# Moving the second FFN's down weight sums from VectorE into adding transfers between DRAM tensors

## The chip, the cores and the metric

The kernel runs on one core of a Trainium2 chip (trn2). The metric is the device time of one execution in microseconds. The kernel before takes 1124.04 us (median of 3 executions, 1123.24 to 1124.38). A difference of about 0.2% (2.25 us) is the least that can be told from no change.

The engines are called as in the profile: PE (TensorE, matmul), PEld (its weight loads), DVE (VectorE), ACT (ScalarE), POOL (GpSimd), SP (SyncE, which here issues nearly all transfers). "L121" is line 121 of the kernel before; the changed kernel has 18 to 24 lines more above most of its code, so there the same line has a higher number.

## The reference

One decoder block on 512 tokens of width 1024, in float32: a SwiGLU feed-forward layer (FFN), a token mixer with two branches, and a second SwiGLU FFN, each between two RMS norms.

```python
def swiglu(x, w_gu, w_down):
    g, u = jnp.split(x @ w_gu, 2, axis=-1)
    return (jax.nn.silu(g) * u) @ w_down

def hybrid_mixer(u, ...):
    z = u @ w_in
    gate_br, x_br, q, k, v, g_lru, g_attn = jnp.split(z, IN_SPLITS, axis=-1)
    xc = causal_depthwise_conv(x_br, conv_w, conv_b)
    y_lru = rg_lru(xc, ...) * jax.nn.gelu(gate_br)
    ...                                   # rotary q and k
    y_attn = sliding_window_attention_with_sinks(q, k, v, attn_sinks)
    merged = jax.nn.sigmoid(g_lru) * (y_lru @ w_proj_lru) + jax.nn.sigmoid(g_attn) * (y_attn @ w_proj_attn)
    return merged @ w_out

def reference(x, ...):
    h = x
    for l in range(DEPTH):                # DEPTH = 1
        f = swiglu(rms_norm(h, ffn1_pre_g[l]), ffn1_w_gu[l], ffn1_w_down[l])
        h = h + MACARON_SCALE * rms_norm(f, ffn1_post_g[l])
        m = hybrid_mixer(rms_norm(h, mix_pre_g[l]), ...)
        h = h + rms_norm(m, mix_post_g[l])
        f = swiglu(rms_norm(h, ffn2_pre_g[l]), ffn2_w_gu[l], ffn2_w_down[l])
        h = h + MACARON_SCALE * rms_norm(f, ffn2_post_g[l])
    return h
```

The inner width of both FFNs is 2816, that is 22 blocks of 128.

## The kernel before, in words

**Products.** Every float32 product is made of three matmuls on a high and a low part of each operand (`mm3`, L150 to L152): high by high, high by low, low by high. A weight block of 128 by 1024 comes from DRAM into one of six buffers (`wload`, L111, issued by SP), ACT writes its high part (L120) and DVE its low part (L121); this is `wsplit`. A fixed list, `worder`, holds all weight blocks in the order in which they are used. Blocks are split two ahead of their use (`AHEAD = 2`), and a block's load is issued once the block six places before it is split (`RAHEAD = 6`). A block of 128 by 1024 feeds 24 matmuls of 512 columns.

**Stages, in order of time in the profiled execution.** First gate and up products of FFN 1 (to about 246 us); down product of FFN 1 (to about 356 us, with the norm that follows); the mixer (to about 785 us); gate and up of FFN 2 (to about 990 us); down of FFN 2 and the last norm (to the end). Inside the mixer come the k and v group, the x group (eight chunks, whose convolution and recurrence are `lru_chunk`), four q chunks (`turn`: rotary), eight chunks of the GeLU gate (`gate_chunk`), four more q chunks, and then eight times a merge gate and a projection (`sig_gate`, `project`), with the attention heads (`attend`) begun beside them.

**The down products and their weight sums.** The down products are made in Strassen's scheme with seven products instead of eight (`strassen_out`). Four of the seven need sums of the quarters of the down weights. With 11 pairs of blocks `c` and `c + 11`, and the halves b11, b12 (block `c`, left and right) and b21, b22 (block `c + 11`), the four sums are s0 = b11 + b12, s1 = s0 + b22, s2 = s1 + b21 and s3 = b12 + b22. They lie in a scratch tensor in DRAM (`t_spill`, one of 128 x 4 x 512 for each pair and FFN), and `worder` takes them from there later, as weight blocks of the products q5, p6, q4 and p7. The sums of both FFNs are formed by the generator `weight_sums` during the first gate and up stage: SP loads two blocks (L283), DVE adds four times (L293), SP stores the sums (L294), 22 times, 11 for each FFN. Only the first FFN's sums are needed soon after.

**What sets the order.** The program is written as interleaved generators: `start` begins one, each call of `tick` lets the running ones count down, and a `yield n` waits for n ticks. In the mixer there is a tick after each product of 24 matmuls (about 5.4 us). The framework then orders the instructions of each engine with a timeline of its own; each engine runs its own list strictly in order, and waits at an instruction until what it needs is there. Buffers come from pools and are handed round: `t2` has 11 buffers of 128 x 512 (the tiles xc, xch, xcl, tr, qa, qb, qw, gp, gls and the attention's ph, pl and c), `t4` has 4 of 128 x 1024 (the attention's scores s, among others), `b8` has 19 of 128 x 2048. The instruction that first writes a new tile into a buffer waits until all readers of the old tile are done.

**POOL before.** POOL does little: the small powers of the norms (L187), and one copy of the sinks into each of the 16 score tiles (`attend`, L918), which waits until the tile's buffer is free.

Of the kernel before, what the change touches and what calls it, by code (L numbers as in the profile page):

```python
# [11 lines left out]
ALU = mybir.AluOpType  # L12
# [4 lines left out]
P = 128  # L17
# [14 lines left out]
KH = KF // 2  # L32
# [11 lines left out]
def hybrid_block_kernel(ctx, tc, x, xt, gcol, gains, gu_first, gu1, dn1, w_x, w_gate, w_kv, w_q, w_gl, w_ga, w_pl,  # L44
# [22 lines left out]
    def b8(name, shape, dtype=F32):  # L67
        return big.tile(shape, dtype, name=name, tag="b8")
# [201 lines left out]
        A.copy(ph[:, i, :], p[:, i, :])  # L270
        V.tensor_tensor(out=pl[:, i, :], in0=p[:, i, :], in1=ph[:, i, :].bitcast(F32), op=ALU.subtract)

    def weight_sums(wait):
        yield wait
        todo_ = [(dn, scratch[f], f, c) for f, dn in enumerate((dn1, dn2)) for c in range(KH)]
        loaded = []

        def load():
            if len(loaded) < len(todo_):
                dn, _, f, c = todo_[len(loaded)]  # L280
                raw = b8(f"tr{f}{c}", [P, 2, 1024])
                for i in range(2):
                    SP.dma_start(raw[:, i, :], dn[c + i * KH])  # L283
                loaded.append(raw)

        load()
        yield 2
        for n, (dn, scr, f, c) in enumerate(todo_):
            raw = loaded[n]
            b11, b12, b21, b22 = (raw[:, i, hc] for i in range(2) for hc in (slice(0, 512), slice(512, 1024)))  # L290
            ts = b8(f"ts{f}{c}", [P, 4, 512])
            for o, a, b in ((0, b11, b12), (1, ts[:, 0], b22), (2, ts[:, 1], b21), (3, b12, b22)):
                V.tensor_tensor(out=ts[:, o], in0=a, in1=b, op=ALU.add)  # L293
            SP.dma_start(scr[c], ts)  # L294
            load()
            yield 1 + n % 4 // 2

    class Blocks:
        def __init__(self, u, name, base, ps):
# [130 lines left out]
    def gate_up(u, name, rows=None, marks=None):  # L430
# [52 lines left out]
        if rows is None:  # L483
            stops.append(base + 2 * block_pairs[0])
            blocks = Blocks(u, name, base, ps)
            extra = blocks.operands(marks)
            first_four(u, f"{name}f", done, marks, extra)
            for _ in extra:
                pass
            blocks.prepare(block_pairs[0])  # L490
        else:
            start(weight_sums(6))
        for j in range(2 if rows is None else 0, KF):
            bb = []
            if j in block_pairs:
# [295 lines left out]
    def lru_chunk(c, b, a4, m4, bx4, last):  # L791
        i = c % 4
        xc = t2(f"xc{c}")
        A.activation(xc, b, AF.Identity, scale=vec[:, 3, c:c + 1], bias=vec[:, 4, c:c + 1])
        for s in range(1, 4):
            V.scalar_tensor_tensor(out=xc[:, s:], in0=b[:, :T - s], scalar=vec[:, 3 - s, c:c + 1], in1=xc[:, s:],
                                   op0=ALU.mult, op1=ALU.add)
        xh, xl = t2(f"xch{c}", F32R), t2(f"xcl{c}", F32R)
        A.copy(xh, xc)
        trail.append(V.tensor_tensor(out=xl, in0=xc, in1=xh.bitcast(F32), op=ALU.subtract))  # L800
        yield LRU_LAG[c // 4]
        cb = slice(c * P, (c + 1) * P)
        br, bi = bank(f"r{c}"), bank(f"i{c}")
        mm3(br, bdt[0][:, 0, cb], bdt[0][:, 1, cb], xh, xl, True, True)
        mm3(bi, bdt[1][:, 0, cb], bdt[1][:, 1, cb], xh, xl, True, True)
        tr = t2(f"tr{c}")
        A.activation(tr, br, AF.Tanh, scale=0.5, bias=hb[:, 0, c:c + 1])
        ti = bx4[:, i, :]
        A.activation(ti, bi, AF.Tanh, scale=0.5, bias=hb[:, 1, c:c + 1])
        V.scalar_tensor_tensor(out=ti, in0=ti, scalar=1.0, in1=xc, op0=ALU.add, op1=ALU.mult)  # L810
        A.activation(a4[:, i, :], tr, AF.Exp, scale=nsp[:, c:c + 1], bias=nsp[:, c:c + 1])
        A.activation(tr, tr, AF.Tanh, scale=nsp[:, c:c + 1], bias=nsp[:, c:c + 1])
        A.activation(m4[:, i, :], a4[:, i, :], AF.Square)
        V.scalar_tensor_tensor(out=m4[:, i, :], in0=m4[:, i, :], scalar=1.0, in1=tr, op0=ALU.add, op1=ALU.mult)
        if not last:
            return
        yield LRU_END[c // 4]
        V.tensor_scalar_min(m4, m4, 0.0)
        A.activation(m4, m4, AF.Sqrt, scale=-0.25)
        for i in range(4):  # L820
            yield 1
            with tc.issue_after(gated[-1].ins) if gated else nullcontext():
                V.tensor_tensor(out=bx4[:, i, :], in0=bx4[:, i, :], in1=m4[:, i, :], op=ALU.mult)
                V.tensor_tensor_scan(out=m4[:, i, :], data0=a4[:, i, :], data1=bx4[:, i, :], initial=0.0,
                                     op0=ALU.mult, op1=ALU.add)
# [3 lines left out]
    def x_group(gi):  # L829
        a4, m4, bx4 = (b8(f"{n}{gi}", [P, 4, T]) for n in ("la", "lm", "lb"))  # L830
        hl.append(m4)
        cr = range(4 * gi, 4 * gi + 4)
        for c in cr:
            w = wget()
            b = bank(f"x{c}")
            feat_chunk(b, w, u2, ALL)
            tick()
            start(lru_chunk(c, b, a4, m4, bx4, c == cr[-1]))

    def qkv_block(b, t, kk, w):  # L840
        for k2 in range(2):
# [57 lines left out]
    def turn(b, name, qh, ql):  # L899
        za, zb, zw = (t2(f"{n}{name}") for n in ("qa", "qb", "qw"))  # L900
        V.tensor_tensor(out=za, in0=b, in1=csq[:, 0], op=ALU.mult)
        trail.append(V.tensor_tensor(out=zb, in0=b, in1=csq[:, 1], op=ALU.mult))
        for i in range(4):
            SP.dma_start(zw[(i ^ 1) * 32:(i ^ 1) * 32 + 32, :], zb[i * 32:i * 32 + 32, :])
        yield 2
        with tc.issue_after(trail[-1].ins) if trail else nullcontext():
            V.tensor_tensor(out=za, in0=za, in1=zw, op=ALU.add)
        A.copy(qh, za)
        V.tensor_tensor(out=ql, in0=za, in1=qh.bitcast(F32), op=ALU.subtract)

    def attend(gi, n, jh, qt, kp, vt, y):
        nm = f"at{gi}{n}{jh}"
        nk = 1 if n == 0 else 2
        W = nk * P
        keys = slice((n - nk + 1) * P, (n + 1) * P)
        s = t4p.tile([P, 4, W + 1], F32, name=f"{nm}s", tag="t4")
        ns = nsink.rearrange("p (a r j i) -> p a r j i", a=2, r=2, j=2)[:, gi, :, jh, :]
        G.tensor_copy(s.rearrange("p (r i) w -> p r i w", r=2)[:, :, :, W], ns)  # L918
        mx, ss = sm(f"{nm}m", 4), sm(f"{nm}ss", 4)
        bs = [bank(f"{nm}b{r}") for r in range(2)]  # L920
        rows = [slice(r * HD, (r + 1) * HD) for r in range(2)]
# [44 lines left out]
    def gate_chunk(c):  # L966
# [6 lines left out]
        A.activation(p, b, AF.Square)  # L973
        gated.append(V.scalar_tensor_tensor(out=p, in0=p, scalar=1.0 / GELU_C, in1=b, op0=ALU.add, op1=ALU.mult))
        trail.append(gated[-1])
        A.activation(p, p, AF.Tanh, scale=SQRT_2_PI * GELU_C)
        V.scalar_tensor_tensor(out=p, in0=p, scalar=1.0, in1=b, op0=ALU.add, op1=ALU.mult)
        V.scalar_tensor_tensor(out=p, in0=p, scalar=0.5, in1=hl[c // 4][:, c % 4, :], op0=ALU.mult, op1=ALU.mult)
# [62 lines left out]
    for c in range(KD):  # L1041
        s = t2(f"gls{c}")
        sig_gate(c, s, "gl")
        b = project(c, yl, "gl")
        if c % 4 == 0:
            m1.append(b8(f"m1{c}", [P, 4, T]))
        V.scalar_tensor_tensor(out=m1[-1][:, c % 4, :], in0=s, scalar=1.0, in1=b, op0=ALU.add, op1=ALU.mult)
        if c == 5:
            start(split_y(ys[0], "ya0"))
        if c in ATT_GL:  # L1050
            next_attend()
# [113 lines left out]
```

## Time and profile before

| | |
|---|---|
| time, median of 3 | 1124.04 us |
| the profiled execution's own time | 1124.64 us |
| its span, first to last instruction | 1122.5 us |
| busy: PE, PEld, DVE, ACT, POOL | 1113.6, 955.4, 838.7, 546.5, 25.0 us |
| granted clock of PE | 0.999 |
| bytes moved by transfers | 192.76 MB |
| DRAM read, written | 160.28 MB, 29.36 MB |
| transfers' share of the 16 DMA engines, hardware queue of SP | 45.1% |

A row of a group reads: line, engine, operation, output<-input by the program's names (buffer numbers left out), shape, count | busy time in us, mean ns of one | idle time of the engine just before, and what ended it. A row of a stretch reads: from:to, length, and for each engine its busy time with the number of its instructions in brackets, then the granted clock of PE, the DMA engines' mean busy share and GB/s. Rows of a timeline begin with the start and the length in us. The span and what lies around it differ by 2.1 us in the profiled execution, which is itself 0.6 us over the median.

### The profile page before, as it was taken

The page shows a single profiled execution, that of the slowest core. Times are in us where ns is not written, and L with a number is a line of the kernel's source. Part 1 is how long each engine was busy: PE and PEld are TensorE (multiplying, and loading weights), DVE is VectorE, ACT ScalarE, POOL GpSimd, SP SyncE. Part 2 cuts the span into 40 slices and gives each one's busy share as a digit, 9 for nine tenths or more (in the row PEclk, how much of TensorE's full clock was granted, in tenths as well). Part 3 has the DMA queues.
Part 4 walks back from the last instruction along what each step waited for, and adds up shares of the span by engine and source line. Part 5 has one row for each costly group of instructions (what it writes and reads, how often), then busy time and mean ns, then how long its engine had stood idle before and what let it go on. Part 6 is the DMA issues. An engine that isn't in the chain of part 4 may idle for free.

```text
span 1122.5 us, 15503 instructions
## 1 busy us (share of the span) xinstructions
PE 1113.6 (99%) x5894; PEld 955.4 (85%) x5894; DVE 838.7 (75%) x1270; ACT 546.5 (49%) x883; POOL 25.0 (2%) x47
## 2 busy tenths in 40 slices
PE   9999999999999999999999999999999999999997
PEld 7888888888888887888888888888999999988886
DVE  5784687778797779797776654646898888868794
ACT  6231221246655478563565554324355565536671
POOL 1000000000010000000000000001000000000001
PEclk9999999999999999999999999999999999999999
DMA  9888989946685322424321222461233233426572
GB/s 361 347 325 314 375 304 355 347 131 195 208 301 186 116 75 70 137 95 131 91 80 39 94 76 75 165 229 61 91 113 112 95 114 102 143 66 213 179 282 76
DMA packets 63963, 192.76 MB, mean 172 GB/s; under 512 B 7824, under 2 KB 8592, under 8 KB 61072
## 3 DMA queue, kind: packets, MB, share of 16 engines
q1 hardware_dynamic: 59136, 176.56, 45.1%
q10 hardware_dynamic: 4752, 15.21, 3.7%
q8 instruction: 46, 0.75, 0.3%
q14 instruction: 29, 0.24, 0.1%
HBM read 160.28 MB, written 29.36 MB: 169 GB/s over the span
## 4 chain that ended last, share of the span: by engine, by line
PE 97%; ACT 2%; DMA 0%; DVE 0%; issue 0%; SPq 0%; POOLq 0%; DVEq 0%
PE f1g L150 7%; PE f1g L151 7%; PE f1g L152 7%; PE f2bx L150 3%; PE f2bx L152 3%; PE f2bx L151 3%; PE f1x L150 2%; PE f1x L152 2%; PE f2x L151 2%; PE f2x L152 2%; PE f2x L150 2%; PE f1x L151 2%; PE glg L150 1%; PE f2by L152 1%; PE f2by L151 1%; PE f2by L150 1%
## 5 line engine op out<-in xcount | busy, mean ns | idle before, releaser
L121 DVE TENSOR_TENSOR w<-wraw,w 128x1024 fp32r<-128x1024 f32 x206 | 239.9, 1184 | 37.0 <-ACT w L120 33.7
L120 ACT CAST w<-wraw 128x1024 fp32r<-128x1024 f32 x206 | 202.3, 1020 | 106.2 <-DVE ts L293 16.2
L150 PE MATMUL f1g<-u1h,w 128*128 128x512 f32 x336 | 130.8, 389 | 0.0
L151 PE MATMUL f1g<-u1l,w 128*128 128x512 f32 x336 | 130.8, 389 | 0.0
L152 PE MATMUL f1g<-u1h,w 128*128 128x512 f32 x336 | 130.7, 389 | 0.0
L152 PEld LDWEIGHTS f1g<-u1h,w 128*128 128x128 f32 x336 | 63.1, 188 | 13.2
L150 PEld LDWEIGHTS f1g<-u1h,w 128*128 128x128 f32 x336 | 63.1, 188 | 13.1
L151 PEld LDWEIGHTS f1g<-u1l,w 128*128 128x128 f32 x336 | 63.1, 188 | 13.0
L468 ACT ACTIVATE f1s<-f1s 128x512 f32<-128x512 f32 x22 | 13.9, 632 | 110.4 <-DVE f1s L467 110.4
L334 DVE TENSOR_TENSOR f2bs<-f2bf,f2bs 128x1024 fp32r<-128x1024 f32 x32 | 39.0, 1221 | 13.0 <-ACT f2bs L334 13.0
L470 DVE SCALAR_TENSOR_TENSOR f1p<-f1s,f1g 128x512 f32<-128x512 f32 x22 | 15.0, 684 | 29.2 <-PE f1g L152 29.1
L334 ACT CAST f2bs<-f2bf 128x1024 fp32r<-128x1024 f32 x32 | 32.0, 1050 | 3.7 <-DVE f2bf L334 3.7
L467 DVE TENSOR_TENSOR f1s<-f1g,rows 128x512 f32<-128x512 f32 x22 | 15.0, 687 | 21.3 <-PE f1g L152 21.1
L293 DVE TENSOR_TENSOR ts<-tr 128x512 f32<-128x512 f32 x44 | 29.5, 684 | 1.1 <-DMA tr<-in_dn_dram 1.1
L293 DVE TENSOR_TENSOR ts<-ts,tr 128x512 f32<-128x512 f32 x44 | 29.8, 683 | 0.3 <-DMA tr<-in_dn_dram 0.3
L334 ACT ACTIVATE f2bs<-f2bg 128x512 f32<-128x512 f32 x16 | 10.1, 634 | 32.7 <-DVE f2bg L334 32.7
L150 PE MATMUL glg<-b1uh,w 128*128 128x512 f32 x64 | 25.8, 403 | 0.0
L150 PE MATMUL glp<-ylh,w 128*128 128x512 f32 x64 | 25.4, 397 | 0.0
L150 PE MATMUL gag<-b1uh,w 128*128 128x512 f32 x64 | 25.4, 396 | 0.0
L150 PE MATMUL q<-b1uh,w 128*128 128x512 f32 x64 | 25.1, 393 | 0.0
L150 PE MATMUL x<-b1uh,w 128*128 128x512 f32 x64 | 25.1, 392 | 0.0
L151 PE MATMUL gag<-b1ul,w 128*128 128x512 f32 x64 | 25.0, 391 | 0.0
(792 smaller groups left out, 3236.2 us busy)
## 6 DMA issues: line engine op xcount, KB each, us to landing
wraw<-in_gu_dram SPq DMA_DIRECT2D x86, 512.0 KB, 4.7
tr<-in_dn_dram SPq DMA_DIRECT2D x44, 512.0 KB, 9.0
t_spill<-ts SPq DMA_DIRECT2D x22, 1024.0 KB, 10.0
wraw<-t_spill SPq DMA_DIRECT2D x88, 256.0 KB, 3.9
wraw<-in_dn_dram SPq DMA_DIRECT2D x66, 256.0 KB, 5.1
wraw<-in_w_x_dram SPq DMA_DIRECT2D x8, 512.0 KB, 4.6
wraw<-in_w_q_dram SPq DMA_DIRECT2D x8, 512.0 KB, 3.4
wraw<-in_w_gate_dram SPq DMA_DIRECT2D x8, 512.0 KB, 3.6
```

What stands on the lines that cost most here:

```text
L120: A.copy(w[:, 0, :end], raws[n][:, :end])
L121: V.tensor_tensor(out=w[:, 1, :end], in0=raws[n][:, :end], in1=w[:, 0, :end].bitcast(F32), op=ALU.subtract)
L150: PE.matmul(o, lhsT=ah, rhs=bh, start=start, stop=False, skip_group_check=more)
L151: PE.matmul(o, lhsT=ah, rhs=bl, start=False, stop=False, skip_group_check=more)
L152: return PE.matmul(o, lhsT=al, rhs=bh, start=False, stop=stop, skip_group_check=more)
L293: V.tensor_tensor(out=ts[:, o], in0=a, in1=b, op=ALU.add)
L334: self.last[key] = fn(*args, **kw)
L467: V.tensor_tensor(out=s, in0=bg, in1=rows, op=ALU.mult)
L468: A.activation(s, s, AF.Tanh, scale=0.5)
L470: V.scalar_tensor_tensor(out=ps[h][-1][:, c % 4, :], in0=s, scalar=0.5, in1=bu, op0=ALU.mult, op1=ALU.mult)
```

## The change

`weight_sums` now forms the sums of one FFN's down weights, and it is started for the first FFN alone: 11 pairs instead of 22 in the first gate and up stage, each with its load, its four adds and its store, at a slower beat (a load, 2 ticks, the adds, 1 tick, the store).

The second FFN's sums are made by a new generator, `weight_sums_dma`, started at the first x chunk of the mixer. It computes nothing on an engine: POOL issues transfers between DRAM tensors. For each of the 11 pairs there are eight, of 128 x 512 (256 KB) each: two plain copies of b12 into s0 and s3; two that add b11 to s0 and b22 to s3 in place; a copy of s0 into s1; one that adds b22 to s1; a copy of s1 into s2; one that adds b21 to s2. So 44 plain copies and 44 adding ones. They are cut into 16 sets, each behind a "beat": a copy by POOL of one column of a tile that the mixer has just made (`beat`, 128 x 1). A set holds one step of up to six pairs, so that a pair's next step comes one set later. The sets have 2, 4, 5, 6, 7, then six times 8, and 6, 4, 3, 2 and 1 transfers, and come 2 and 3 ticks apart in turn. The tiles of the 16 beats are, by the built program, xc0, xc1, xc4, xc6, qb01, gp0, gp3, gp5, gp7, qb11, qb13, gls0, gls2, gls3, gls4 and gls5 (the numbers are the chunks). Each is a `t2` tile, so that the next user of its buffer now waits for POOL as well. A transfer waits for the transfer of the set before whose result it reads or changes, and for the transfer eight places before it, whose semaphore it takes over.

The 16 copies of the sinks go from POOL to DVE.

```diff
@@ -270,30 +270,48 @@
         A.copy(ph[:, i, :], p[:, i, :])
         V.tensor_tensor(out=pl[:, i, :], in0=p[:, i, :], in1=ph[:, i, :].bitcast(F32), op=ALU.subtract)
 
-    def weight_sums(wait):
+    def weight_sums(dn, scr, name, wait):
         yield wait
-        todo_ = [(dn, scratch[f], f, c) for f, dn in enumerate((dn1, dn2)) for c in range(KH)]
-        loaded = []
-
-        def load():
-            if len(loaded) < len(todo_):
-                dn, _, f, c = todo_[len(loaded)]
-                raw = b8(f"tr{f}{c}", [P, 2, 1024])
-                for i in range(2):
-                    SP.dma_start(raw[:, i, :], dn[c + i * KH])
-                loaded.append(raw)
-
-        load()
-        yield 2
-        for n, (dn, scr, f, c) in enumerate(todo_):
-            raw = loaded[n]
+        for c in range(KH):
+            raw = b8(f"{name}tr{c}", [P, 2, 1024])
+            for i in range(2):
+                SP.dma_start(raw[:, i, :], dn[c + i * KH])
+            yield 2
             b11, b12, b21, b22 = (raw[:, i, hc] for i in range(2) for hc in (slice(0, 512), slice(512, 1024)))
-            ts = b8(f"ts{f}{c}", [P, 4, 512])
+            ts = b8(f"{name}ts{c}", [P, 4, 512])
             for o, a, b in ((0, b11, b12), (1, ts[:, 0], b22), (2, ts[:, 1], b21), (3, b12, b22)):
                 V.tensor_tensor(out=ts[:, o], in0=a, in1=b, op=ALU.add)
+            yield 1
             SP.dma_start(scr[c], ts)
-            load()
-            yield 1 + n % 4 // 2
+
+    beat = []
+
+    def weight_sums_dma(dn, scr):
+        parts = [[dn[c + i * KH][:, hc] for i in range(2) for hc in (slice(0, 512), slice(512, 1024))] for c in range(KH)]
+
+        def add(o, src):
+            G.dma_start(o, src, accum_op=ALU.add)
+
+        for n in range(KH + 5):
+            with tc.issue_after(G.tensor_copy(sm("beat"), beat[-1]).ins):
+                for lag in range(min(n, 5), max(0, n - KH + 1) - 1, -1):
+                    b11, b12, b21, b22 = parts[n - lag]
+                    t = [scr[n - lag][:, i] for i in range(4)]
+                    if lag == 0:
+                        G.dma_start(t[0], b12)
+                        G.dma_start(t[3], b12)
+                    elif lag == 1:
+                        add(t[0], b11)
+                        add(t[3], b22)
+                    elif lag == 2:
+                        G.dma_start(t[1], t[0])
+                    elif lag == 3:
+                        add(t[1], b22)
+                    elif lag == 4:
+                        G.dma_start(t[2], t[1])
+                    else:
+                        add(t[2], b21)
+            yield 2 + n % 2
 
     class Blocks:
         def __init__(self, u, name, base, ps):
@@ -489,7 +507,7 @@
                 pass
             blocks.prepare(block_pairs[0])
         else:
-            start(weight_sums(6))
+            start(weight_sums(dn1, scratch[0], name, 6))
         for j in range(2 if rows is None else 0, KF):
             bb = []
             if j in block_pairs:
@@ -798,6 +816,7 @@
         xh, xl = t2(f"xch{c}", F32R), t2(f"xcl{c}", F32R)
         A.copy(xh, xc)
         trail.append(V.tensor_tensor(out=xl, in0=xc, in1=xh.bitcast(F32), op=ALU.subtract))
+        beat.append(xc[:, :1])
         yield LRU_LAG[c // 4]
         cb = slice(c * P, (c + 1) * P)
         br, bi = bank(f"r{c}"), bank(f"i{c}")
@@ -836,6 +855,8 @@
             feat_chunk(b, w, u2, ALL)
             tick()
             start(lru_chunk(c, b, a4, m4, bx4, c == cr[-1]))
+            if c == 0:
+                start(weight_sums_dma(dn2, scratch[1]))
 
     def qkv_block(b, t, kk, w):
         for k2 in range(2):
@@ -900,6 +921,7 @@
         za, zb, zw = (t2(f"{n}{name}") for n in ("qa", "qb", "qw"))
         V.tensor_tensor(out=za, in0=b, in1=csq[:, 0], op=ALU.mult)
         trail.append(V.tensor_tensor(out=zb, in0=b, in1=csq[:, 1], op=ALU.mult))
+        beat.append(zb[:, :1])
         for i in range(4):
             SP.dma_start(zw[(i ^ 1) * 32:(i ^ 1) * 32 + 32, :], zb[i * 32:i * 32 + 32, :])
         yield 2
@@ -915,7 +937,7 @@
         keys = slice((n - nk + 1) * P, (n + 1) * P)
         s = t4p.tile([P, 4, W + 1], F32, name=f"{nm}s", tag="t4")
         ns = nsink.rearrange("p (a r j i) -> p a r j i", a=2, r=2, j=2)[:, gi, :, jh, :]
-        G.tensor_copy(s.rearrange("p (r i) w -> p r i w", r=2)[:, :, :, W], ns)
+        V.tensor_copy(s.rearrange("p (r i) w -> p r i w", r=2)[:, :, :, W], ns)
         mx, ss = sm(f"{nm}m", 4), sm(f"{nm}ss", 4)
         bs = [bank(f"{nm}b{r}") for r in range(2)]
         rows = [slice(r * HD, (r + 1) * HD) for r in range(2)]
@@ -973,6 +995,7 @@
         A.activation(p, b, AF.Square)
         gated.append(V.scalar_tensor_tensor(out=p, in0=p, scalar=1.0 / GELU_C, in1=b, op0=ALU.add, op1=ALU.mult))
         trail.append(gated[-1])
+        beat.append(p[:, :1])
         A.activation(p, p, AF.Tanh, scale=SQRT_2_PI * GELU_C)
         V.scalar_tensor_tensor(out=p, in0=p, scalar=1.0, in1=b, op0=ALU.add, op1=ALU.mult)
         V.scalar_tensor_tensor(out=p, in0=p, scalar=0.5, in1=hl[c // 4][:, c % 4, :], op0=ALU.mult, op1=ALU.mult)
@@ -1045,6 +1068,7 @@
         if c % 4 == 0:
             m1.append(b8(f"m1{c}", [P, 4, T]))
         V.scalar_tensor_tensor(out=m1[-1][:, c % 4, :], in0=s, scalar=1.0, in1=b, op0=ALU.add, op1=ALU.mult)
+        beat.append(s[:, :1])
         if c == 5:
             start(split_y(ys[0], "ya0"))
         if c in ATT_GL:
```

The order of PE's instructions is unchanged. On DVE, in the first gate and up stage (an early stretch of it, beside the splits of the weight blocks that were loaded as wraw_392 and after; ts are the sums, w the low parts of the weight blocks, f1s the gate), before:

```order
L293 TENSOR_TENSOR ts_645<-ts_645,tr_576 128x512
L121 TENSOR_TENSOR w_615<-wraw_392,w_615 128x1024
L121 TENSOR_TENSOR w_659<-wraw_430,w_659 128x1024
L293 TENSOR_TENSOR ts_645<-ts_645,tr_576 128x512
L293 TENSOR_TENSOR ts_719<-tr_651 128x512
L121 TENSOR_TENSOR w_689<-wraw_460,w_689 128x1024
L121 TENSOR_TENSOR w_733<-wraw_504,w_733 128x1024
L467 TENSOR_TENSOR f1s_654<-f1g_590,rows_175 128x512
L293 TENSOR_TENSOR ts_719<-tr_651 128x512
```

and of the change:

```order
L283 TENSOR_TENSOR f1ts_597<-f1ts_597,f1tr_528 128x512
L121 TENSOR_TENSOR w_602<-wraw_392,w_602 128x1024
L283 TENSOR_TENSOR f1ts_701<-f1tr_633 128x512
L121 TENSOR_TENSOR w_641<-wraw_430,w_641 128x1024
L283 TENSOR_TENSOR f1ts_597<-f1ts_597,f1tr_528 128x512
L121 TENSOR_TENSOR w_671<-wraw_460,w_671 128x1024
L283 TENSOR_TENSOR f1ts_701<-f1tr_633 128x512
L121 TENSOR_TENSOR w_711<-wraw_500,w_711 128x1024
L485 TENSOR_TENSOR f1s_636<-f1g_572,rows_175 128x512
```

The adds and the splits now alternate, and half of the adds are gone from the stage as a whole (88 before, 44 now).

On POOL, in the mixer's last q chunks and first merge gates (beat copies, then the transfers between the inputs' `in_dn2_dram` and the scratch `t_spill1`), of the change; before, only the copies at L918 stood there:

```order
L296 COPY beat_4151<-qb11_4113 128x1
L293 DMA t_spill1_4_93<-in_dn2_dram 128x512
L311 DMA t_spill1_5_94<-t_spill1_5_94 128x512
L293 DMA t_spill1_6_95<-in_dn2_dram 128x512
L301 DMA t_spill1_9_98<-in_dn2_dram 128x512
L302 DMA t_spill1_9_98<-in_dn2_dram 128x512
L307 DMA t_spill1_7_96<-t_spill1_7_96 128x512
L293 DMA t_spill1_8_97<-in_dn2_dram 128x512 x2
L296 COPY beat_4308<-qb13_4225 128x1
L293 DMA t_spill1_5_94<-in_dn2_dram 128x512
```

A beat's copy (L296) stands behind all transfers of the set before.

On DVE, in the second group of q chunks, of the change (the copies at L940 are the sinks' copies that stood on POOL; at020s is a score tile):

```order
L923 TENSOR_TENSOR qb_4113<-q_4087,csq 128x512
L121 TENSOR_TENSOR w_4121<-wraw_3805,w_4121 128x1024
L929 TENSOR_TENSOR qa_4073<-qa_4073,qw_4075 128x512
L931 TENSOR_TENSOR ql_4032<-qa_4073,qh_4031 128x512
L940 COPY at020s<-nsink 128x4
L121 TENSOR_TENSOR w_4234<-wraw_3895,w_4234 128x1024
L968 TENSOR_TENSOR at000pl_4167<-at000t_4161,at000ph_4166 128x512
L922 TENSOR_TENSOR qa_4173<-q_4126,csq 128x512
L923 TENSOR_TENSOR qb_4174<-q_4126,csq 128x512
```

Before, the same rows stand in the same order without the copy. The copy waits for the buffer of an older score tile, and a split (L121) now stands right behind it.

## The prediction

> **What bounds the kernel now.** First the page's busy times and the waits of PE:
>
> ```profile
> PE 1113.6 (99%) x5894; PEld 955.4 (85%) x5894; DVE 838.7 (75%) x1270; ACT 546.5 (49%) x883; POOL 25.0 (2%) x47
> PE warm L183 <- POOL ident masks.py:199: 1.4, 1, 1.4
> PE r L150 <- ACT xch L799: 0.6, 1, 0.6
> PE f1g L710 <- ACT u1h L700: 0.6, 1, 0.6
> PE f2by L152 <- DVE f2bs L334: 0.2, 1, 0.2
> ```
>
> PE is busy nearly throughout, and all its waits come to 2.8 us, of which 2.0 (warm, L710) lie in the first 8 us. A busy PE need not be at its peak, so next the stretches: does PE's pace depend on what the change lightens?
>
> ```profile
> 84.00:112.00 28.00, 28.00 (x125) 23.19 (x124) 13.91 (x20) 5.15 (x6) 0.00 (x0) 1.00 0.82 315
> 112.00:140.00 28.00, 28.00 (x125) 23.19 (x124) 17.64 (x27) 5.89 (x7) 0.00 (x0) 1.00 0.97 379
> 140.00:168.00 28.00, 28.00 (x125) 23.17 (x124) 23.69 (x33) 7.95 (x9) 0.00 (x0) 1.00 0.86 299
> 28.00:240.00 212.00, 212.00 (x939) 175.52 (x938) 151.31 (x225) 54.49 (x65) 0.00 (x0) 1.00 0.83 317
> ```
>
> It doesn't. In the first gate and up stage DVE is busy 13.91 or 23.69 us of 28, and the transfers' share is 0.82 or 0.97: PE does 125 matmuls each time, at the full granted clock, and it is never idle from 28 to 240 us. So the stage that loses work has nothing to give back. The stage that gains work is the mixer:
>
> ```profile
> 434.00:448.00 14.00, 13.36 (x57) 10.22 (x56) 13.93 (x19) 11.36 (x18) 0.00 (x0) 1.00 0.29 94
> 476.00:490.00 14.00, 14.00 (x63) 11.61 (x62) 14.00 (x20) 4.84 (x9) 0.00 (x0) 1.00 0.21 76
> 462.00:532.00 70.00, 70.00 (x331) 57.59 (x330) 58.42 (x102) 35.42 (x64) 1.17 (x2) 1.00 0.35 112
> 532.00:604.00 72.00, 72.00 (x446) 61.22 (x445) 55.00 (x167) 42.88 (x119) 1.97 (x6) 1.00 0.25 81
> ```
>
> Here DVE is full in places (13.93 and 14.00 of 14 us), and at 434 us its lateness already reaches PE. From 462 to 604 us it has 11.6 and 17.0 us free, and the transfers' share is low.
>
> **The change part by part.** *Removed: 44 adds of DVE in the first stage.*
>
> ```profile
> L293 DVE TENSOR_TENSOR ts<-ts,tr 128x512 f32<-128x512 f32 x44 | 29.8, 683 | 0.3 <-DMA tr<-in_dn_dram 0.3
> L293 DVE TENSOR_TENSOR ts<-tr 128x512 f32<-128x512 f32 x44 | 29.5, 684 | 1.1 <-DMA tr<-in_dn_dram 1.1
> tr<-in_dn_dram SPq DMA_DIRECT2D x44, 512.0 KB, 9.0
> t_spill<-ts SPq DMA_DIRECT2D x22, 1024.0 KB, 10.0
> L294 SPq DMA_DIRECT2D t_spill<-ts x22: 320/326/360, 45.5 to 218.5; - x22
> L111 SPq DMA_DIRECT2D wraw<-t_spill x88: 319/323/1633, 239.7 to 1061.5; - x88
> ```
>
> Half of 88 adds is 44 x 0.684 = 30.1 us of DVE, with 22 loads and 11 stores on SP. All of it lay under PE's matmuls: worth 0 us. At the slower beat the last pair of FFN 1 comes after 6 + 11 x 3 = 39 ticks, 39 x 24 x 0.226 = 211 us after the start, about where the last store stood (218.5 us; 0.226 is 212 us over 939 matmuls). It lands some 10 us later, ahead of the first read of the sums (239.7 us): 0 us.
>
> *Moved: 16 copies of the sinks, POOL to DVE.* DVE has no such copy in this trace; its nearest row is the reciprocal of the same shape, and what matters more is when a score buffer comes free, which stands in POOL's row:
>
> ```profile
> 505.98 0.17 DVE L935 RECIPROCAL at001ss<-at001ss 128x4 f32<-128x4 f32 x1
> L918 POOL COPY at020s<-nsink x1: 977/977/977, 518.0 to 518.0; 128x4 f32<-128x4 f32 x1
> L918 POOL COPY at111s<-nsink x1: 999/999/999, 595.8 to 595.8; 128x4 f32<-128x4 f32 x1
> 515.82 0.69 DVE L909 TENSOR_TENSOR ql<-qa,qh 128x512 fp32r<-128x512 f32 x1 [0.74 <-ACT qh L908]
> ```
>
> 16 x 0.17 = 2.7 us, at most 16 x 1.0 by POOL's longest. On DVE the copy at020s waits from the end of the ql before it (516.5) to 518.0, 1.5 us, with a split of weights queued behind it. That split is two blocks ahead, 48 matmuls or 10.9 us, so PE doesn't notice. I take 0 us, and keep 16 us in the free time above as the upper end, which still is hidden.
>
> *Added: 16 beats and 88 transfers on POOL.* No transfer issued by POOL stands in the trace. Two prices are unknown, POOL's time for one issue, c, and the time to landing, L. Rows:
>
> ```profile
> L187 POOL TENSOR_TENSOR b3qpr<-b3qpe,mhalf 128x1 f32<-128x1 f32 x4 | 6.1, 1530 | 324.9 <-DVE b3qpe L229 324.9
> DMA to landing us min/median/max: 3.0/4.0/12.4
> DMA to landing us min/median/max: 4.3/9.0/13.4
> ```
>
> For c: below, SP's issue (0.32 us); above, POOL's slowest group (1.53). For L: 4.0 us is the median of the reads of the sums, 9.0 and at most 13.4 that of the loads tr in the crowded first stage. What do they have to beat? A beat reads a tile, and the next user of that tile's buffer waits for it. The tightest places:
>
> ```profile
> 479.44 0.68 DVE L974 SCALAR_TENSOR_TENSOR gp<-gp,gt 128x512 f32<-128x512 f32 x1
> 512.66 0.68 DVE L902 TENSOR_TENSOR qb<-q,csq 128x512 f32<-128x512 f32 x1
> 525.70 0.68 DVE L902 TENSOR_TENSOR qb<-q,csq 128x512 f32<-128x512 f32 x1
> 570.47 0.57 ACT L988 ACTIVATE gls<-glg 128x512 f32<-128x512 f32 x1
> 580.19 1.29 DVE L946 TENSOR_TENSOR at021pl<-at021t,at021ph 128x512 fp32r<-128x512 f32 x2
> ```
>
> These are gp3 (done at 480.1), qb11 (done at 513.3), qb13, which takes qb11's buffer (525.7), gls3 (571.0), and the second at021pl, which takes that of gls3 (580.8). So the beat on qb11 may come 12.4 us late and that on gls3 9.8 us. By c: behind the beat on gp3 stand three sets of eight before the copy on qb11 is due, so 24c + 1 must fit into 525.7 - 480.1 = 45.6 us: c up to 1.85 us. Up to gls3 it is 5 x 8 + 6 + 4 = 50 transfers in 100.7 us, c up to 2.0. By L: each set waits for the one before, seven steps from gp3 to gls3, so L + c up to 14.3 us. With c between 0.32 and 1.53 and L at 4 or 9, both hold, and POOL's lateness costs 0 us; only both upper ends together (1.53 + 13.4 = 14.9) miss. I take c near 1.0, between its ends, and L at 4 to 9, since the share here is 0.25 to 0.35.
>
> *Late end.* The 88 issues end by 604 + a few us, or, at c = 2.7, 88 x 2.7 = 238 us after the first beat (384 us). The second FFN's first read of its sums is far behind:
>
> ```profile
> 1004.80 5.46 SPq L111 DMA_DIRECT2D wraw<-t_spill  x5
> ```
>
> **Sum.** 1124.64 (the profiled execution) + 0 + 0 + 0, and the median of the runs is 0.6 below it: 1124.0. For DVE's few us of new waits around the stall at 434 us I add 0.2: **1124.2 us**.
>
> **The rivals.** *A, slower: the DMA engines can't carry a set in time, and POOL falls behind.* A copy reads and writes 262 KB of DRAM, an add reads twice and writes once: a set of eight is 4 x 2 + 4 x 3 = 20 such pieces, 5.24 MB. If they share the highest rate in the trace (379 GB/s) with the 112 GB/s of the stretch, a set takes 5.24 / 0.267 = 19.6 us, 2.45 us for a transfer: over 1.85, so it decides. At gls3 the lateness is 50 x 2.45 - 100.7 = 22 us; less the 10.9 that the splits are ahead, PE loses 11: 1135. Against it: the trace counts a load's byte once,
>
> ```profile
> q1 hardware_dynamic: 59136, 176.56, 45.1%
> ```
>
> and by this row (176.56 MB in 506 us, 349 GB/s) eight transfers of 262 KB take 6.0 us, or 9.0 if an add counts twice, of a set's 12.8 (five sets in the 64 us from gp0 to qb13). That fits, closely. The Trainium skill, DMA: Bandwidth & Descriptors, Specifications, gives DRAM about 358 GB/s for one core; the stretch at 112 us moved 379, so the trace goes above it. By that limit a set would take 21 us and the time would be about 1145.
>
> *B, slower: DVE waits for the rotary's small transfers.* Between 445 and 530 us each `qa` add waits for four transfers `qw<-qb`, issued by SP:
>
> ```profile
> 508.80 2.41 SPq L904 DMA_DIRECT2D qw<-qb  x4
> DMA to landing us min/median/max: 1.9/2.0/3.9
> 514.39 0.69 DVE L907 TENSOR_TENSOR qa<-qa,qw 128x512 f32<-128x512 f32 x1
> ```
>
> The last is issued by 511.2, lands at 513.2, and is wanted at 514.4: 1.2 us to spare. If landing rises to the 9.0 of the crowded stage, each of four chunks waits 5.8 us, 23.2 in all, against 11.6 us free (less 2.7) and 10.9 of lead: 3.4 us on PE, 1127.5. It decides from 7 us on. Against it: the share only reaches the crowded 0.8 if A's bytes hold.
>
> *C, faster.* The freed DVE would have to shorten PE's path. PE's waits after 8 us sum to 0.8, and the starts around 434 us are stretched by some tenths: at most 1.1 us, 1123.0, below what can be told.
>
> *D: the sums come too late for FFN 2.* That needs a transfer to take over 7 us of POOL (620 us over 88). Nothing points to it.
>
> **How the numbers follow.** The forecast (hidden on both sides, C included) 0.66, A 0.16, B 0.13, D 0.01, and 0.04 for a gain that no row shows. The forecast alone spans 1123.0 to 1126; to leave out no more than 2 in 10 the range takes in B and the gentle part of A: 1122.9 to 1130. Faster by over 0.2% 0.04, within 0.2% (2.25 us) 0.66, slower 0.30.
>
> **What would show it.** In the profile of the changed kernel: PE without idle time from 28 to 240 us and DVE some 30 us less busy there; 88 transfers in POOL's rows at about 1 us each and landing under 10 us; beats on qb11 and gls3 less than 12 and 9 us behind their tiles; no wait of DVE, ACT or SP for POOL over 2 us; DVE's `qa` adds waiting under 2 us each. A transfers' share near 1.0 from 462 to 532 us, with DVE waiting for POOL at `qb` or the attention's `pl`, would speak for A, long waits for `qw` for B. The prediction is wrong if PE is idle for more than 2 us in all between 383 and 650 us, or if the time falls below 1122.

## The result and the profile after

The change makes the kernel slower. Beside runs of the kernel before on the same chips, its median was 1132.82 us against 1124.11 (ratio 1.0076, 95% interval 1.0057 to 1.0094), and in a second comparison 1131.67 against 1123.70 (1.0072, 1.0059 to 1.0085). The forecast was 1124.2, its range ended at 1130.0.

| | before | after |
|---|---|---|
| median, first comparison | 1124.11 us | 1132.82 us |
| profiled execution / its span | 1124.64 / 1122.5 us | 1130.32 / 1128.3 us |
| PE idle, 462 to 604 us | 0 | 4.9 us |
| DVE busy, 28 to 240 us | 151.3 us | 126.4 us |
| DMA share, 462 to 532 and 532 to 604 us | 0.35, 0.25 | 0.95, 0.99 |
| median landing of `qw<-qb` | 2.0 us | 7.6 us |

Stretches of the changed kernel first (columns as in the prediction: length, then PE, weight loads, DVE, ACT and POOL busy with their counts, granted clock, DMA share, GB/s):

```profile
28.00:240.00 212.00, 212.00 (x938) 175.54 (x937) 126.39 (x181) 54.15 (x65) 0.00 (x0) 1.00 0.57 208
462.00:532.00 70.00, 69.30 (x327) 56.72 (x326) 54.85 (x96) 31.56 (x58) 22.40 (x34) 1.00 0.95 217
532.00:604.00 72.00, 67.83 (x417) 56.85 (x416) 51.97 (x153) 40.47 (x106) 23.56 (x38) 1.00 0.99 206
```

The stage that lost work gained nothing: PE is busy for all of its 212 us, with as many matmuls as before, although DVE is 25 us less busy and the transfers' share fell from 0.83 to 0.57. (The 44 adds last 0.684 us each, 30.1 in all, but overlap their neighbours a little; hence 25.) The loss lies in the mixer. There the DMA engines are now full, and PE is idle for 0.70 and 4.17 us where it never was: 4.9 of the 5.8 us by which the span grew. Whom did PE wait for, and whom did those wait for? The waits of PE, then of DVE, then of ACT in the changed kernel (us in all, times, longest):

```profile
PE at030t L965 <- DVE at021pl L968: 1.8, 1, 1.8
PE glp L152 <- DVE w L121: 1.4, 1, 1.4
PE glg L150 <- ACT gls L1011: 0.8, 1, 0.8
PE gt L150 <- ACT w L120: 0.7, 1, 0.7
```

```profile
DVE qa L929 <- DMA qw<-qb: 12.2, 3, 5.7
DVE at021pl L968 <- POOL beat L296: 6.7, 1, 6.7
DVE qb L923 <- POOL beat L296: 5.0, 1, 5.0
```

```profile
ACT at020ph L967 <- POOL beat L296: 4.8, 1, 4.8
```

Two ways lead to PE. **A**: a beat comes late, so the buffer that it reads stays taken, and DVE and ACT, whose next tile goes there, wait 16.5 us for POOL. The two places of DVE are those that the prediction named as the tightest: `qb` (qb13 takes qb11's buffer) and `at021pl` (it takes gls3's). **B**: the rotary's transfers land late, and DVE waits 12.2 us at its `qa` adds. What POOL itself did: its waits, the rows of two of its lines (duration min/median/max in ns), and two beats in the timeline (start and length in us):

```profile
POOL t_spill L293 <- issue: 49.5, 27, 4.9
POOL t_spill L301 <- issue: 16.7, 7, 4.5
POOL t_spill L307 <- issue: 10.0, 7, 3.4
```

```profile
L293 POOL DMA_DIRECT2D t_spill<-in_dn_dram x44: 804/836/1452, 389.1 to 610.8; - x44
DMA to landing us min/median/max: 5.3/8.4/11.7
...
L301 POOL DMA_DIRECT2D t_spill<-in_dn_dram x11: 540/555/1176, 383.3 to 567.9; - x11
```

```profile
568.99 0.20 POOL L296 COPY beat<-gls 128x1 f32<-128x1 f32 x1
...
592.38 0.20 POOL L296 COPY beat<-gls 128x1 f32<-128x1 f32 x1
```

An issue takes 0.55 us (plain, L301) or 0.84 (an add, L293), and a transfer lands after 8.4 us: both inside the bounds of the prediction. Yet POOL sits 76 us between issues waiting for something that the profile does not name, and the beat on gls3, a tile done at 571.0 in the kernel before, comes at 592.4. From the beat on gp3 (488.75 us) to that on gls0 (568.99) it issues five sets of eight: 16.0 us a set, 2.0 us a transfer.

### The profile page after: what moved, and what is told of

Read it like the earlier page. It is cut to its first block, busy times and chain, and to the rows that moved or that the text cites. A ratio compares the mean times of both kernels' runs of the same rounds, so it can differ in the third digit from the quotient of the medians.

```text
span 1128.3 us, 15514 instructions
## 1 busy us (share of the span) xinstructions
PE 1114.4 (99%) x5894; PEld 955.0 (85%) x5894; DVE 813.9 (72%) x1242; ACT 545.2 (48%) x883; POOL 87.4 (8%) x135
## 4 chain that ended last, share of the span: by engine, by line
PE 85%; issue 6%; POOL 3%; DVE 2%; ACT 2%; DMA 1%; SPq 0%; POOLq 0%; DVEq 0%; ACTq 0%
PE f1g L152 7%; PE f1g L150 7%; PE f1g L151 7%; PE f2bx L150 3%; PE f2bx L152 3%; PE f2bx L151 3%; POOL t_spill L293 2%; PE f1x L151 2%; PE f1x L152 2%; PE f2x L151 2%; PE f2x L152 2%; PE f2x L150 2%; PE f1x L150 2%; PE f2by L152 1%; PE f2by L151 1%
## 5 line engine op out<-in xcount | busy, mean ns | idle before, releaser
L121 DVE TENSOR_TENSOR w<-wraw,w 128x1024 fp32r<-128x1024 f32 x206 | 240.0, 1183 | 34.3 <-ACT w L120 30.7
L293 POOL DMA_DIRECT2D t_spill<-in_dn_dram x44 | 37.9, 891 | 60.1 <-issue 49.5
L187 POOL TENSOR_TENSOR b3qpr<-b3qpe,mhalf 128x1 f32<-128x1 f32 x4 | 6.1, 1530 | 324.7 <-DVE b3qpe L229 324.7
L187 POOL TENSOR_TENSOR b1qpr<-b1qpe,mhalf 128x1 f32<-128x1 f32 x4 | 2.8, 709 | 319.1 <-DVE b1qpe L229 319.1
L152 PE MATMUL glp<-ylh,w 128*128 128x512 f32 x64 | 25.1, 392 | 1.4 <-DVE w L121 1.4
L150 PE MATMUL gt<-b1uh,w 128*128 128x512 f32 x64 | 25.0, 391 | 0.7 <-ACT w L120 0.7
L150 PE MATMUL glp<-ylh,w 128*128 128x512 f32 x64 | 25.4, 397 | 0.0
```

Of the source, the lines that this page charges most:

```text
L121: V.tensor_tensor(out=w[:, 1, :end], in0=raws[n][:, :end], in1=w[:, 0, :end].bitcast(F32), op=ALU.subtract)
L150: PE.matmul(o, lhsT=ah, rhs=bh, start=start, stop=False, skip_group_check=more)
L152: return PE.matmul(o, lhsT=al, rhs=bh, start=False, stop=stop, skip_group_check=more)
L187: G.tensor_tensor(out=r, in0=ms, in1=mhalf, op=ALU.pow)
L293: G.dma_start(o, src, accum_op=ALU.add)
```

## The experiments

Ratios are to the kernel before, run beside each.

### Are the transfers the whole cause?

```diff
-                for lag in range(...):   # the 88 transfers
+                pass
...
-        worder += [down_item(dn, scratch[f], prod, c) ...]
+        worder += [down_item(dn, scratch[0], prod, c) ...]
```

> The changed kernel with its beats, its copies on VectorE and its slower pace, but without the 88 transfers; FFN 2 reads FFN 1's sums instead, by as many loads of the same size (output not the reference's). If the transfers are the whole cause, 1124.0 +-1 us; if the copies on VectorE, the beats or the pace cost something, over 1126.

Measured: 1124.04 us, 1.0004 (0.9995 to 1.0013). FFN 2 reads FFN 1's sums here, so its loads stay. DVE's copies of the sinks, the beats and FFN 1's slower pace cost nothing that shows (at most 0.13% by the interval), and the 44 adds that are gone bring nothing. The whole loss is that of the transfers.

### A and B, each alone

Beats that hold no buffer (A taken away, B left):

```diff
+    marks_ = const.tile([P, 32], mybir.dt.bfloat16, name="marks")
+    def mark(E, x):                       # by the engine that wrote x
+        m = marks_[:, len(beat) % 32:len(beat) % 32 + 1]
+        (E.copy if E is A else E.tensor_copy)(m, x)
+        beat.append(m)
...
-        beat.append(zb[:, :1])
+        mark(V, zb[:, :1])                # and so for xc, gp, gls
```

> The changed kernel, but every beat reads a column of a small tile of its own, which ScalarE or VectorE copies out of the beat's tile as soon as that is written; so a late POOL holds no buffer. Two ways in which late transfers can reach TensorE are in the changed kernel's profile: (A) late beats hold buffers (16.5 us of waits of VectorE and ScalarE for POOL; PE idle 2.4 us at 583 to 593 us), (B) the rotary's transfers land late (12.2 us of waits of VectorE; PE idle 2.3 us around 538 to 546 us). If A and B share the loss as PE's idle time does, 1128 to 1129 us; if A is all, 1124 to 1125; if B is all, 1132 to 1134.

No rotary transfers (B taken away, A left):

```diff
-        for i in range(4):
-            SP.dma_start(zw[(i ^ 1) * 32:(i ^ 1) * 32 + 32, :], zb[i * 32:i * 32 + 32, :])
...
-            V.tensor_tensor(out=za, in0=za, in1=zw, op=ALU.add)
+            V.tensor_tensor(out=za, in0=za, in1=zb, op=ALU.add)
```

> The changed kernel without the 32 rotary transfers qw<-qb: the add takes qb as it stands, unswapped (output not the reference's). Mechanism B is gone, A remains. If A and B share the loss, 1128 to 1129 us; if B is all, 1124 to 1125; if A is all, 1132 to 1134.

Both edits:

> Both at once: beats on tiles of their own, and no rotary transfers (output not the reference's). If A and B are the whole loss, 1124 to 1125 us, although the transfers are as slow as before; if late weights or the moved copies take part, over 1126 us.

And the change itself beside them:

> The changed kernel itself once more, beside the next two, to see whether A alone (beats that hold buffers) and B alone (late rotary transfers) add up to the change's loss. A alone cost 0.33% and B alone 0.18%: if they only add up, 1129.5 us (0.5%); if each eats the other's slack, 1132 to 1134 us, as first measured (0.76%).

| kernel | A | B | median | ratio (95%) |
|---|---|---|---|---|
| the change, again | yes | yes | 1131.67 us | 1.0072 (1.0059 to 1.0085) |
| no rotary transfers | yes | no | 1126.74 us | 1.0033 (1.0020 to 1.0045) |
| own marks | no | yes | 1126.05 us | 1.0018 (1.0009 to 1.0028) |
| both edits | no | no | 1123.74 us | 1.0001 (0.9991 to 1.0010) |

With A and B gone no loss is left, and in that kernel the transfers are nearly as slow and the engines nearly as full as in the change. Its rows for the two stretches and for the landing of POOL's transfers:

```profile
462.00:532.00 70.00, 70.00 (x330) 57.63 (x330) 59.75 (x116) 35.81 (x65) 23.90 (x37) 1.00 0.98 223
532.00:604.00 72.00, 72.00 (x447) 61.22 (x446) 55.22 (x173) 43.36 (x123) 21.46 (x34) 1.00 0.91 196
```

```profile
t_spill<-in_dn_dram POOLq DMA_DIRECT2D x66, 256.0 KB, 7.7
t_spill<-t_spill POOLq DMA_DIRECT2D x22, 256.0 KB, 8.5
```

So full DMA engines alone did not slow PE, and weights that land late didn't either (in this kernel those of the merge gates, `w_gl`, land after 8.9 us, against 3.6 before). What costs is that something on the path waits for a transfer (B) or for the engine that issues them (A). A alone came to 0.33%, B alone to 0.18%; their intervals overlap, so which is larger is not shown. In the kernel without rotary transfers DVE and ACT still wait 15.3 us for POOL at beats (16.5 in the change), so A is there nearly whole; but `qw`'s buffers stay unused in it, so the tiles that follow in them have less to wait for, and 0.33% may be a little under A's price. Both expectations had each of them near 1128 to 1129 and were too high; together the two give 0.51%, the change 0.72 and 0.76%. That each eats the slack of the other is suggested by this, but the intervals (0.2 to 0.45 and 0.09 to 0.28 for the parts) do not exclude a plain sum, and 1131.67 lies between the two values expected. Of B's 2 us the profiled execution, the second shortest of its ten at 1125.08, shows little: 0.2 us of waits of PE, at `gt`. Where the rest lies is open.

### What makes the sets slow?

The adds as plain copies, all of them, and then the last two of each column's four:

```diff
-            G.dma_start(o, src, accum_op=ALU.add)
+            G.dma_start(o, src)
```

> The changed kernel with its 44 adding transfers as plain copies of the same 262 KB (the sums are wrong). In the changed kernel's trace an add holds the 16 DMA engines for 1.91 us and a plain copy for 1.10 us, so a set of eight goes from 12.1 to at most 8.8 us. If the DMA engines' time is what makes the sets late, a set now fits into its 12.8 us beside the other transfers (share 0.35): the loss shrinks by more than half, 1124 to 1127 us, and POOL's 77 us of unexplained waits shrink too. If it is the number of transfers (POOL's issue, the waits between them), nothing changes: 1130 to 1134.

```diff
                     elif lag == 3:
-                        add(t[1], b22)
+                        G.dma_start(t[1], b22)
...
                     else:
-                        add(t[2], b21)
+                        G.dma_start(t[2], b21)
```

> Of each column's four adding transfers the last two are plain copies (the sums are wrong). By the times that the DMA engines are held, a set of eight takes 2 x 1.91 + 6 x 1.10 = 10.4 us instead of 12.0 (all adds) or 8.8 (none), of the 12.8 us that it has, beside 0.35 x 12.8 = 4.5 us for the others. If the loss begins where the engines are full, it lies clearly nearer to no loss than to the change's, since lateness only costs beyond the slack: 1124 to 1127 us. If each add had its own price, half the loss: 1128 to 1129.

Measured: 1123.81 us (1.0001, 0.9992 to 1.0011) without adds, and 1124.47 (1.0009, 1.0000 to 1.0018) with half of them. The row of POOL's queue (packets, MB, share of the 16 DMA engines over the span) of the change, of the kernel with half of the adds and of that without, in this order:

```profile
q0 software_dynamic: 9856, 23.07, 11.9%
```

```profile
q0 software_dynamic: 8448, 23.07, 9.7%
```

```profile
q0 software_dynamic: 7040, 23.07, 7.7%
```

The bytes counted are the same, the engines' time is not. 7.7% of 1122.5 us is 86.4 us, 0.98 for each of 88 plain copies of 262 KB. In the change it is 134.3 us; less 44 plain ones at 0.98, an add takes (134.3 - 43.1) / 44 = 2.07 us. The kernel between bears that out: 22 x 2.07 + 66 x 0.98 = 110.2 us, and the row gives 0.097 x 1122.5 = 108.9. The expectations' 1.91 and 1.10 are the same thing told apart by the size of the packets, within the change's own trace. So an add costs as much as 1.7 to 2.1 copies, and a set of four and four 4 x 3.05 = 12.2 us of all 16 engines. Of its cadence of 12.8 us the other transfers' share of 0.35 leaves it 8.3.

By this sum a set of plain copies fits (8 x 0.98 = 7.8 us), and one with half of the adds (10.0) does not.

The number of transfers and of beats is the same in all three, so it is not those. An issue takes POOL 0.52 us at L293 without adds, not 0.84, but that is 1.3 us for a set of eight; and the landing there hardly moves (7.7 us against 8.4). What moves is how late POOL comes. The rows of the beats on gls (first and last start in us) in the kernel without transfers, without adds, with half of the adds, and in the change, in this order:

```profile
L296 POOL COPY beat<-gls x5: 185/186/268, 529.0 to 602.6; 128x1 f32<-128x1 f32 x5
L296 POOL COPY beat<-gls x5: 183/273/973, 541.9 to 603.6; 128x1 f32<-128x1 f32 x5
L296 POOL COPY beat<-gls x5: 185/198/426, 551.1 to 603.8; 128x1 f32<-128x1 f32 x5
L296 POOL COPY beat<-gls x5: 197/273/482, 569.0 to 610.2; 128x1 f32<-128x1 f32 x5
```

The first of them is 13, 22 and 40 us late. Yet no engine waits for POOL at a beat without adds or with half of them, and POOL's unnamed waits without adds are 11 us, not 76. The price is not by the add either: half of the adds cost about an eighth of the loss, 0.09% of 0.72. Nor is it by full engines alone, since from 503 to 532 us the share is 1.02 without adds and 1.01 with half. By these rows the loss begins where a beat is later than the next user of its tile's buffer can bear.

A row of DVE's waits in the kernel without adds warns about B:

```profile
DVE qa L929 <- DMA qw<-qb: 11.8, 4, 4.4
```

These are 11.8 us of waits for the rotary, nearly as in the change (12.2), and no loss of time. With own marks 10.4 us of such waits came with a loss of 0.18%, which went when the rotary's transfers did. So the length of these waits doesn't tell what they cost; why they cost in the one kernel and not in the other is open.

### The unexplained waits of POOL

```diff
-    nc = _bacc.Bacc("TRN2", ..., dynamic_dma_scratch_size=1024)
+    nc = _bacc.Bacc("TRN2", ..., dynamic_dma_scratch_size=3072)
...
-    csq = const.tile([P, 2, T], F32, name="csq")
+    csq = const.tile([P, 1, T], F32, name="csq")
```

> The changed kernel with three times the space for the descriptors of POOL's transfers (3072 bytes instead of 1024; room is made by halving the rotary's table, both halves then read alike, so the output is not the reference's and one load of 256 KB is gone). POOL waits 77 us between issues for nothing that the profile shows. If that is for room for descriptors, these waits go to nearly nothing. If that room is also what makes the sets late, 1124 to 1127 us; if the DMA engines are full anyway (share 1.0 from 503 to 560 us), the landing times grow or POOL waits for the transfers before instead, and the time stays 1129 to 1134.

Measured: 1130.72 us, 1.0061 (1.0046 to 1.0076), as slow as the change within the intervals. POOL's waits in this kernel, the longest and the unnamed ones, and its landings at L293:

```profile
POOL t_spill L293 <- DMA t_spill<-t_spill: 30.9, 11, 6.2
POOL t_spill L311 <- DMA t_spill<-in_dn_dram: 13.2, 7, 4.7
POOL t_spill L293 <- issue: 0.6, 3, 0.3
POOL t_spill L307 <- issue: 0.6, 2, 0.4
```

```profile
DMA to landing us min/median/max: 4.9/10.5/18.0
```

The unnamed waits, 76 us in the change, are 1.2 us now: POOL waited for room for descriptors (what its transfers are written down in; the program sets the space for them). But that was a symptom. With room, the transfers queue in the engines instead (10.5 us to landing, at most 18.0, against 8.4 and 11.7), and POOL waits for the set before.

### Spread out, and the copies put back

```diff
...
+    SETS = (0, 3, 6, 12, 16, 20, 24, 26, 27, 29, 30, 32, 35, 38, 42, 45)
...
+        if len(beat) - 1 in SETS and sets_:     # in mark(): one set at this mark
+            next(sets_[0], None)
```

> Everything computed as in the changed kernel, but the 16 sets stand 18 to 30 us apart instead of 13, from 383 to about 735 us, each released by a mark of its own. If it is the density that hurts, 1124 to 1125 us, as before the change, with an add landing in under 6 us and the DMA share under 0.9 in each stretch; if a transfer among the stage's others hurts however sparse, above 1127.

Measured: 1124.17 us, 1.0005 (0.9995 to 1.0014): all that the change computes, at the old time. In its trace the beats stand 14 to 34 us apart, from 383 to 728 us. Its two stretches, and the landing of its rotary transfers:

```profile
462.00:532.00 70.00, 70.00 (x331) 57.65 (x330) 56.86 (x111) 32.72 (x60) 15.76 (x24) 1.00 0.78 188
532.00:604.00 72.00, 72.00 (x447) 61.23 (x446) 58.20 (x178) 46.14 (x130) 18.07 (x28) 1.00 0.79 169
```

```profile
qw<-qb SPq DMA_DIRECT2D x32, 64.0 KB, 3.3
```

The rotary's transfers land in 3.3 us. Two details of the expectation were wrong: an add still lands after 8.0 us (presumably behind the others of its own set), and one stretch, 604 to 640 us, still has a share of 0.94, where nothing on the path waits for it. This version also has the marks, so it doesn't tell how much of the cure is the spacing alone. It is no faster than the kernel before: the freed 25 us of DVE are not on the path.

```diff
-        V.tensor_copy(s.rearrange("p (r i) w -> p r i w", r=2)[:, :, :, W], ns)
+        G.tensor_copy(s.rearrange("p (r i) w -> p r i w", r=2)[:, :, :, W], ns)
```

> The changed kernel with the 16 copies of the sinks back on POOL, where they queue behind the transfers. If the moved copies were part of the loss, faster than 1130 us; if the move was needed, the copies come up to 18 us late, VectorE's masking waits for them, and it is slower than the changed kernel, 1136 to 1150 us.

Measured: 1145.00 us, 1.0186 (1.0169 to 1.0203). The move to VectorE was needed. The copy into at030s, for one, comes 23 us later than in the change (564.3), and it is ACT that waits for it, not VectorE's masking. The longest wait of PE, and from the rows on the copies one that came late and who waited for it:

```profile
PE at100b L947 <- ACT gls L1011: 13.6, 1, 13.6
```

```profile
L940 POOL COPY at030s<-nsink x1: 476/476/476, 587.7 to 587.7; 128x4 f32<-128x4 f32 x1
...
ACT at030s L956: 21.9, 1
```

## Why the prediction was wrong, point by point

- **The first stage: right.** 0 us for 44 adds fewer, by the stretch (PE busy 212.00 of 212 us in both) and by the kernel without transfers. FFN 1's last adds start at 206.3 us and its sums are stored well before they are read, as worked out (211).
- **The moved copies: right.** 0.16 us each on DVE (0.17 was taken), worth 0.
- **POOL's price and the landing: right as numbers, wrong as a test.** Taken were c near 1.0 and L at 4 to 9 us; measured are 0.55 and 0.84, and 8.4. Both bounds that were derived from them (c up to 1.85 us, L + c up to 14.3) hold, and POOL fell behind all the same. The step that failed is the one that let a transfer cost POOL no more than its issue: "so 24c + 1 must fit into 525.7 - 480.1 = 45.6 us", from which "POOL's lateness costs 0 us" followed. Transfers of one set were taken to fly side by side for nothing, though they share 16 engines. In place of c belonged the time for which a transfer holds these engines, 1.53 us on average (134.3 / 88), and with the other transfers beside it 2.0 as it ran, over the limit of 1.85. The prediction's own sign of being wrong, PE idle for more than 2 us, came with 4.9 from 462 to 604 us.
- **The argument against rival A: here the chance was lost.** A set was priced at 6.0 us of the engines, or 9.0 if an add counts twice, by the loads' row (349 GB/s), and "That fits, closely". It measured 12.2. That an add counts twice was about right (2.07 against 0.98); a plain copy was mis-sized, 0.98 us and not the 0.75 of a load. And with the others' share of 0.35 (4.5 us of 12.8) even 9.0 did not fit, 13.5 of 12.8; the share had been quoted and was not added. The 12.8 is a mean, too: in the kernel without transfers the five beats from gp3 to the first gls have 42.8 us (486.2 to 529.0), 8.6 each.
- **The time at gp3 was off too.** The beat was taken to be free when the tile's first gate product is done (480.1). It reads the tile after its last write, at 488.6 in the changed kernel, released by DVE's L1001. That takes some 7 us from the 45.6 and brings the limit from 1.85 down to about 1.6.

```profile
488.75 0.98 POOL L296 COPY beat<-gp 128x1 f32<-128x1 f32 x1 [10.21 <-DVE gp L1001]
536.36 0.69 DVE L923 TENSOR_TENSOR qb<-q,csq 128x512 f32<-128x512 f32 x1 [5.04 <-POOL beat L296]
592.62 0.69 DVE L968 TENSOR_TENSOR at021pl<-at021t,at021ph 128x512 fp32r<-128x512 f32 x1 [6.73 <-POOL beat L296]
```

- **Rival A: right in mechanism and place, near in its time by luck.** It took 2.45 us for a transfer and put the beat on gls3 22 us behind the time when the buffer is wanted (580.8 in the kernel before). The beat came at 592.4, 11.6 behind. The sum made of the 22 a loss of 11, to 1135; A alone cost 3.0 (1126.74 against 1123.72). That 1135 lies near the change's 1131.7 to 1132.8 comes of a price that was too high and of B, which it left out. It had 0.16.
- **Rival B: right in mechanism, its wait over-sized.** It was to decide from 7 us of landing on, and 7.6 was measured; but its own sum (four waits against 8.9 us free and 10.9 of lead) decides only from 8.1 on, so at 7.6 it gave no loss. DVE's waits were put at 23.2 us and came to 12.2; its time at 1127.5, against 1126.05 alone. The 1.2 us to spare were those of one chunk: the last of the four already waits 2.0 us in the kernel before.
- **The chances.** A and B were written as alternatives, with 0.29 between them. They have one cause, transfers that are late because the DMA engines are full, and come together; the case "both" was missing. Each alone stays inside the range (1126.74 and 1126.05 against 1130.0), and both together leave it.
- **Rivals C and D: rightly small.** PE gained nothing, and the last transfer was issued at 610.8 us, some 400 before the sums are read.
- **The page's limit.** The prediction gave a sentence to the 358 GB/s that the Trainium skill, DMA: Bandwidth & Descriptors, Specifications, sets for one core's DRAM: 21 us for a set, 1145 us. A set took 16.0 us. The clearest row on this is in the kernel without adds, from 490 to 520 us (packets, MB, share of the 16 engines of POOL's queue and of SP's):

```profile
q0 software_dynamic: 1499, 4.93, 65.5%
q1 hardware_dynamic: 1065, 3.10, 32.3%
```

A counted byte of POOL's stands for a read and a write there, and 0.52 MB of SP's are the rotary's and don't touch DRAM: 12.4 MB moved in 30 us, 415 GB/s, so the limit did not bind. In the change (3.65 and 3.13 MB from 503 to 532 us, 0.79 of them the rotary's) it was some 395 GB/s if an add reads twice, and some 333 if it reads once, as the profile's count of bytes read has it. Both are below 415, so nothing here points to the DRAM as what held the change.

## What to carry to other kernels

Price a batch of transfers by the time for which it holds the DMA engines, add the share that is already in use, and compare the sum with the cadence; what goes beyond it costs once the slack of the next users is used up. This comes before the issuing engine's time and the landing of a single one, which can both look harmless. An operation that uses a tile only as a sign that it is time should not hold the tile: with a column copied aside, the same late transfers cost a quarter of what the change cost. And rivals that share a cause belong in one case, with the price of both.

## What was not expected of the hardware

An add in a transfer from DRAM to DRAM held the DMA engines for 2.07 us per 262 KB, a plain copy for 0.98 (127 and 268 GB/s), beside the other transfers of these kernels.

A wait of PE can cost more than its length. In the second profile of the change PE waits 2.85 us, and afterwards its granted clock is halved for a while (two rows of its timeline, then three stretches):

```profile
585.96 0.29 PE L947 MATMUL at101b<-kp,qh 64*128 64x128 f32 x1 [2.85 <-DVE at020pl L968]
...
588.60 0.63 PE L152 MATMUL glg<-b1uh,w 128*128 128x512 f32 x1
589.02 0.63 PE L150 MATMUL glg<-b1uh,w 128*128 128x512 f32 x1
```

```profile
582.00:587.00 5.00, 1.85 (x24) 1.46 (x24) 1.88 (x4) 2.44 (x6) 1.60 (x3) 1.00 1.07 324
587.00:590.50 3.50, 3.50 (x14) 2.80 (x13) 1.62 (x4) 0.44 (x1) 1.85 (x3) 0.51 1.05 180
590.50:604.00 13.50, 13.50 (x79) 11.63 (x79) 9.20 (x36) 8.40 (x26) 3.47 (x7) 1.00 0.92 116
```

For 3.5 us a matmul starts every 0.42 us and not every 0.227: some 1.7 us on top of the wait. The Trainium skill, TensorE: Matmul & The Clock Gate, Part 1, says that the clock is at half after an idle window of about 3.4 us, and at full again after a busy one of that length. The length of the slow stretch agrees. The wait before it does not: 2.85 us here; and in the kernel without rotary transfers two waits of 1.1 us together were enough, by its row of PE's waits and the stretch behind them, while 1.8 us in the first profile of the change were not. From which wait on it happens is open.

```profile
PE at101b L945 <- DVE at020pl L966: 1.1, 2, 0.8
```

```profile
580.00:584.60 4.60, 4.48 (x20) 3.65 (x21) 2.25 (x5) 1.01 (x2) 1.36 (x2) 0.63 1.01 190
```

This would explain why the profiled execution of the change, with a clock of 1.00 throughout, is the shortest of its four (1130.3 us against 1132.2 to 1133.9 at mean clocks of 0.994 to 0.998); the traces of the others were not kept, so that is argued and not shown, and the shortest execution of the second comparison, 1129.67 us at 0.997, does not fit it well.
